# One layer of a hybrid streaming encoder: the DeltaNet heads' convolution copies on another engine, and their transposes placed at other k-tiles

## The chip, the core and the metric

The kernel runs on one core of one Trainium2 chip. The time is that of one execution on the device in microseconds; the median of three runs of the kernel before is 2997.08 us (2996.59 to 2997.41). One further execution was taken by the hardware profiler, and all rows in this document are from such profiled executions.

The core's engines each work through a queue of their own in order: PE (TensorE, matrix products and transposes; PEld is its weight load), DVE (VectorE), ACT (ScalarE), POOL (GpSimd) and SP, which only issues DMAs. They wait for one another through semaphores.

## The reference

One layer over 512 prompt frames and 64 sample frames, width 2048, all in float32. Cut to what matters here (the DeltaNet half, "GDN"; there is also a gated linear attention half, "GLA", and a gated feed-forward network behind both):

```python
mod = silu(c) @ w_ada + b_ada                       # 2048 x 12288, both conditions
h = rmsnorm(x, norm1) * (1 + sc1) + sh1
proj = h @ w_in                                     # 2048 x 7200
qkv, conv_new = causal_dwconv(concat([b_q, b_k, b_v]), st_conv, gdn_conv_w)   # 4 taps
qkv = silu(qkv)
q = l2norm(heads(c_q)) * 128 ** -0.5;  k = l2norm(heads(c_k));  v = heads(c_v)
...
lower = where(strict, einsum(kb, k) * decay, 0)     # per block
sol = triangular_solve(eye + lower, concat([v * beta, kb * exp(G)]))
u = sol_v - sol_k @ S
o = (q * exp(G)) @ S + (einsum(q, k) * decay) @ u
S = exp(G_last) * S + (k * exp(G_last - G)).T @ u
...
o = rmsnorm(o) * gain * silu(b_g)
x = x + g1 * (concat([o_gla, o_gdn]) @ w_out);  h = rmsnorm(x, norm2) * (1 + sc2) + sh2
x = x + g2 * ((silu(causal_dwconv(gate) + b) * val) @ w_down)
```

There are eight GDN heads of 128 columns. `conv_new`, the last three frames of the convolution's input for the prompt and for the sample, is an output.

## The kernel before

**Products.** Each float32 product is made of three products of a rounded upper half and a lower half: `split` loads a weight tile, ACT rounds it (L595, `wh`), DVE takes the rest (L596, `wl`), and `mm6` issues per k-tile of 128 six matmuls (two halves of the 576 frames, three products). `in_tile` makes one tile of 128 columns of the input projection from 16 k-tiles, and after each k-tile calls `tick`.

**Jobs.** The recurrence of a head runs as a Python generator (a job) between these k-tiles. `tick` calls `job_step` once per k-tile. It goes through the open jobs, the oldest first, and resumes each until one did work: a job that gives back `WAIT` lets the next one have the step as well. `rest(n)` gives back `WAIT` n times, so it is a pause of n k-tiles, longer where an older job works in between. `tick` also advances the modulation's blocks for later (`ada_block`, DVE at L738 and PE at L744).

`gdn_heads` makes the head's tiles in the order q(h+1), k(h+1), v(h), gate(h), 64 k-tiles a head; for head 0, q and k come from the stage before. After k(h) the job of head h is opened, so two jobs overlap. q, k and v each go through `gdn_conv`: ACT and DVE copy the projection out of PSUM into `cb` (L880, L881), with three columns in front of the prompt (zeros) and three in front of the sample (the state) from POOL (L882, L883); POOL copies the last three columns of both into `cs` (L884, L885); then ACT scales by the first tap (L886), DVE adds three taps (L888) and ACT applies Silu into the head's tile (L890) and the sample's (L891).

**The steps of a job** (`gdn`), where a `yield` ends a step:

- load of the decay rows `gb` by SP (L166), the masks `dl` and `du` on ACT (Relu, Exp) and POOL (`affine_select`, L174, L175);
- transposes of the raw keys (`transpose4`, L140, four per call, into one of four PSUM banks `bank`), squares on ACT, `rsqrt` (DVE adds at L133, POOL takes the power -1/2 at L134), scaled keys `kT`; one step; the same for the queries, of which only the lengths are kept; `rest(REST_T)`;
- `kn`, the transposes of `kT`; one step; `a` = keys by keys with the mask (L212); one step; keys by queries (L218); one step;
- `inverse16`: SP stores `a` to DRAM and loads its 16 x 16 diagonal blocks (a store and four loads), `rest(8)`, 14 steps with two POOL operations each (L343 to L350), a store (L351) and two loads on SP, two DVE operations that spread the result (L358), `rest(16)`;
- eight steps that double the inverse's block size to 128 (L234, L240, L249, L254);
- once the head's v is there: its transposes, then four blocks with two or three steps each (L272 to L301), whose outputs ACT collects in `ops`;
- squares of `ops`, `rsqrt`, scaling; `rest(REST_N)`; transposes of `ops` (L140), gain, gate, store.

A ninth job does the sample's frames of all heads, four GLA jobs and their sample job follow.

**Order.** The order on each engine's queue is fixed at compile time by the framework from priorities (program order) and its own estimate of durations; `high_priority` (AHEAD for weights, JOB_AHEAD for the jobs' ACT and DVE operations) moves instructions ahead by 80 places.

Helper lines: the jobs' ACT and DVE operations all carry L1584, so the tiles tell them apart (`m`, `sq`, `s`, `rq`). The widths of the pauses and the powers stand in these lines:

```python
REST_D, REST_X, REST_T, REST_N, REST_G = 8, 16, 3, 2, 3
self.nc.vector.tensor_scalar_add(out[:parts, :n], src[:parts, :n], EPS)
self.nc.gpsimd.tensor_tensor(out[:parts, :n], out[:parts, :n], self.mhalf[:parts, :n], op=ALU.pow)
```

Of the kernel before, what the change touches and what calls it, by code (L numbers as in the profile page):

```python
# [8 lines left out]
F32 = mybir.dt.float32  # L9
F32R = mybir.dt.float32r  # L10
I32 = mybir.dt.int32
AF = mybir.ActivationFunctionType
# [4 lines left out]
P = 128  # L17
# [14 lines left out]
JOB_RATE, ADA_RATE = 1.0, 0.65  # L32


REST_D, REST_X, REST_T, REST_N, REST_G = 8, 16, 3, 2, 3
LATE = 3
N_EARLY = 4
N_EXTRA = 24
# [53 lines left out]
class Kern:  # L92
# [58 lines left out]
    def gdn(self, qF, kF, x, gain, hcols, gb_src, s0, s_out, o_put, last_level):  # L151
# [7 lines left out]
        nc, c = self.nc, self.c  # L159
        V, A, T = self.jv, self.ja, nc.tensor  # L160
# [19 lines left out]
            A.activation(dl[:, b], dl[:, b], AF.Copy, scale=nbeta[:, b:b + 1])  # L180


        ss, rr = self.small(8), self.small(8)
        junk = self.half()
        kps = self.transpose4(kF)
        for b in range(4):
            A.activation(junk, kps[:, b], AF.Square, accum_out=ss[:, b:b + 1])
        self.rsqrt(rr, ss, 4)
        kT = self.m4()
        for b in range(4):  # L190
            A.activation(kT[:, b], kps[:, b], AF.Copy, scale=rr[:, b:b + 1])
        yield
        ss, rq = self.small(8), self.sp.tile([P, 4], F32, tag="rq", bufs=3, name=self.name("rq"))
        qps = self.transpose4(qF)
        for b in range(4):
            A.activation(junk, qps[:, b], AF.Square, accum_out=ss[:, b:b + 1])
        self.rsqrt(rq, ss, 4)
        V.tensor_scalar_mul(rq, rq, float(P) ** -0.5)
        yield from self.rest(REST_T)

        kn = self.m4()
# [21 lines left out]
        u, t = yield from self.inverse16(a)  # L223
# [83 lines left out]
        ss, rr = self.small(8), self.small(8)  # L307
        junk = self.half()
# [565 lines left out]
    def gdn_conv(self, ps, t, dst, name, h):  # L874

        nc = self.nc
        V, A = nc.vector, nc.scalar
        cb = self.ap.tile([P, 582], F32, tag="cb", bufs=1, name=self.name("cb"))
        acc = self.ap.tile([P, 582], F32, tag="ca", bufs=1, name=self.name("ca"))
        A.activation(cb[:, 3:515].rearrange("p (h t) -> p h t", h=2), ps[:, :, :HP], AF.Copy)  # L880
        V.tensor_copy(cb[:, 518:582].rearrange("p (h t) -> p h t", h=2), ps[:, :, HP:HT])  # L881
        nc.gpsimd.tensor_copy(cb[:, 0:3], self.zero3)  # L882
        nc.gpsimd.tensor_copy(cb[:, 515:518], self.vmap["st_conv"].rearrange("p (i t) -> p t i", i=3)[:, t])  # L883
        nc.gpsimd.tensor_copy(self.cs[:, 0, :, t], cb[:, 512:515])  # L884
        nc.gpsimd.tensor_copy(self.cs[:, 1, :, t], cb[:, 579:582])  # L885
        A.activation(acc[:, :579], cb[:, 0:579], AF.Copy, scale=self.vec("gdn_conv_w", t))  # L886
        for j in range(1, 4):
            V.scalar_tensor_tensor(acc[:, :579], cb[:, j:j + 579], self.vec("gdn_conv_w", 24 * j + t), acc[:, :579],  # L888
                                   op0=ALU.mult, op1=ALU.add)
        A.activation(dst, acc[:, 0:512], AF.Silu)  # L890
        self.put_s(name, h, lambda s: A.activation(s, acc[:, 515:579], AF.Silu))  # L891

    def put_o(self, k, t):
# [601 lines left out]
def layer_kernel(tc, i, o):  # L1495
    nc = tc.nc
    with ExitStack() as ctx:
        K = Kern(tc, ctx, i, o)
# [14 lines left out]
        with ExitStack() as early:  # L1513
            K.wp = pool(early, "wp", "right", bufs=3)
            with ExitStack() as right:
# [8 lines left out]
                K.mp = right.enter_context(_MixPool(tc))  # L1524
                with ExitStack() as st:
                    K.ap = pool(st, "ap", bufs=1)
                    K.jobs, K.at_job, K.at_ada = [], 0.0, 0.0
                    K.dp = dp
                    acc = [lambda n=n: K.ap.tile([P, 512], F32, tag=f"acc{n}", bufs=1, name=K.name("acc")) for n in range(2)]
# [116 lines left out]
```

## Time and profile before

| | |
|---|---|
| median of three runs | 2997.08 us |
| the profiled execution's own time | 3002.07 us |
| its span, first to last instruction | 3000.3 us |
| mean granted PE clock | 0.987 |
| busy: PE, DVE, ACT, POOL | 2912.2, 2095.7, 1242.9, 307.3 us |

The stages by time in the profile: the modulation, the norm and the first projections to about 150 us; the GDN heads to about 850; the GLA heads and half of the output projection to about 1400; the feed-forward network to the end.

How to read the rows. A group has its line, engine, operation, tiles (written `<-` read, buffer numbers left out), shapes and count, then busy time in us, mean ns of one, and the engine's idle time just before, with what ended it. A timeline row has start and duration in us, engine, line, operation and count, and in brackets the idle time before it with what ended that wait. A row of the waits has the waiting engine, tile and line, the releaser, then us in total, times and the longest. "PEq" or "SPq" is an engine's sequencer. "Granted clock" is the share of full speed that the throttle grants PE.

### The profile page before, as it was taken

How to read it: one execution, taken by the hardware profiler on the slowest of the kernel's cores; microseconds unless marked ns; L12 is line 12 of the kernel's file. 1: busy time of each engine (PE TensorE's matmuls, PEld its weight loads, DVE VectorE, ACT ScalarE, POOL GpSimd, SP SyncE). 2: the span in 40 equal slices, each digit the busy share in tenths (PEclk: the TensorE clock that was granted, in tenths of full speed). 3: DMA queues.
4: the chain of work that ended last, by engine and by line, in shares of the span. 5: the costliest groups of instructions: out<-in, count | busy, mean ns of one | idle time of the engine just before them, and what ended most of it. 6: DMA issues, size and time to landing. Idle time of an engine off the chain costs nothing.

```text
span 3000.3 us, 52414 instructions
## 1 busy us (share of the span) xinstructions
PE 2912.2 (97%) x21128; PEld 2796.7 (93%) x21128; DVE 2095.7 (70%) x3226; ACT 1242.9 (41%) x2116; POOL 307.3 (10%) x610
## 2 busy tenths in 40 slices
PE   7988999999999999999999999999999999999998
PEld 3588899999999998999999999999999999999998
DVE  5776667776578777367888888888888865555555
ACT  6555444554343333255444444444444432212223
POOL 0033333332200000000000000000000000000000
PEclk9999999999999999999999999999999999999999
DMA  7844545554455456543333333333333473333221
GB/s 274 283 142 134 148 121 149 144 152 134 133 144 145 135 159 172 153 143 96 97 111 105 106 98 111 106 104 99 112 104 104 122 238 101 116 101 106 89 85 65
DMA packets 532599, 392.95 MB, mean 131 GB/s; under 512 B 58729, under 2 KB 463204, under 8 KB 532356
## 3 DMA queue, kind: packets, MB, share of 16 engines
q1 hardware_dynamic: 532356, 389.59, 43.5%
q8 instruction: 167, 2.74, 0.4%
q14 instruction: 76, 0.62, 0.1%
HBM read 355.16 MB, written 34.36 MB: 130 GB/s over the span
## 4 chain that ended last, share of the span: by engine, by line
PE 65%; DVE 2%; DMA 1%; ACT 1%; issue 1%; POOL 0%; SPq 0%; ACTq 0%; POOLq 0%; DVEq 0%
PE g L508 19%; PE g L510 10%; PE g L1261 8%; PE g L1262 8%; PE g L1263 8%; PE bank L1262 3%; PE bank L1261 3%; PE bank L1263 3%; PE bank L401 1%; DVE acc L738 0%; PE bank L140 0%; PE bank L744 0%; PE bank L1471 0%; POOL s L134 0%; DMA xr<-od 0%
## 5 line engine op out<-in xcount | busy, mean ns | idle before, releaser
L508 PE MATMUL g<-slot,wh 128*128 128x288 f32 x3168 | 551.9, 295 | 0.2 <-DVE slot L1031 0.2
L1261 PE MATMUL g<-slot,wh 128*128 128x290 f32 x1760 | 533.6, 303 | 2.4 <-ACT p L1273 2.4
L1262 PE MATMUL g<-slot,wh 128*128 128x290 f32 x1760 | 526.1, 299 | 0.0
L1263 PE MATMUL g<-slot,wl 128*128 128x290 f32 x1760 | 521.2, 296 | 0.0
L595 ACT ACTIVATE wh<-raw 128x1024 fp32r<-128x1024 f32 x223 | 235.4, 1058 | 613.6 <-PE g L508 596.7
L508 PEld LDWEIGHTS g<-slot,wh 128*128 128x128 f32 x3168 | 466.2, 188 | 0.7 <-DVE slot L1031 0.5
L508 PE MATMUL g<-hh,wh 128*128 128x288 f32 x1984 | 453.7, 307 | 1.9 <-DVE cb L881 1.5
L510 PE MATMUL g<-hh,wl 128*128 128x288 f32 x1984 | 443.9, 302 | 3.4 <-DVE wl L596 3.4
L508 PE MATMUL g<-hl,wh 128*128 128x288 f32 x1984 | 439.8, 301 | 0.0
L1031 DVE SCALAR_TENSOR_TENSOR slot<-g,mod,slot 128x512 f32<-128x512 f32 (+1 forms) x448 | 201.9, 492 | 308.9 <-PE g L510 304.7
L738 DVE SCALAR_TENSOR_TENSOR acc<-xr,ct,acc 128x512 f32<-128x512 f32 x480 | 340.0, 754 | 35.4 <-DMA xr<-in_w_ada_dram 34.8
L1208 ACT ACTIVATE wh<-raw 128x1024 fp32r<-128x1024 f32 x176 | 186.7, 1061 | 393.5 <-PE g L1262 389.1
L1261 PEld LDWEIGHTS g<-slot,wh 128*128 128x128 f32 x1760 | 331.1, 188 | 16.7 <-ACT p L1273 11.5
L510 PE MATMUL g<-slot,wl 128*128 128x288 f32 x1584 | 343.2, 295 | 0.0
L1263 PEld LDWEIGHTS g<-slot,wl 128*128 128x128 f32 x1760 | 336.5, 191 | 0.0
L1262 PEld LDWEIGHTS g<-slot,wh 128*128 128x128 f32 x1760 | 334.6, 190 | 0.1
L508 PEld LDWEIGHTS g<-hh,wh 128*128 128x128 f32 x1984 | 324.3, 191 | 5.7 <-issue 1.6
L510 PEld LDWEIGHTS g<-hh,wl 128*128 128x128 f32 x1984 | 324.8, 191 | 4.3 <-DVE wl L596 3.7
L508 PEld LDWEIGHTS g<-hl,wh 128*128 128x128 f32 x1984 | 324.7, 191 | 1.0 <-issue 0.7
L596 DVE TENSOR_TENSOR wl<-raw,wh 128x1024 fp32r<-128x1024 f32 x223 | 272.3, 1222 | 58.6 <-ACT wh L595 57.9
L510 PEld LDWEIGHTS g<-slot,wl 128*128 128x128 f32 x1584 | 254.9, 188 | 0.0
L1209 DVE TENSOR_TENSOR wl<-raw,wh 128x1024 fp32r<-128x1024 f32 x176 | 214.9, 1221 | 19.8 <-ACT wh L1208 19.3
(367 smaller groups left out, 4415.7 us busy)
## 6 DMA issues: line engine op xcount, KB each, us to landing
raw<-in_w_up_dram SPq DMA_DIRECT2D x176, 512.0 KB
xr<-in_w_ada_dram SPq DMA_DIRECT2D x128, 512.0 KB
raw<-in_w_in_dram SPq DMA_DIRECT2D x108, 512.0 KB
raw<-in_w_down_dram SPq DMA_DIRECT2D x88, 512.0 KB
hraw<-in_w_ada_dram SPq DMA_DIRECT2D x64, 512.0 KB
raw<-in_w_out_dram SPq DMA_DIRECT2D x32, 512.0 KB
slot<-actd SPq DMA_DIRECT2D x44, 288.0 KB
actd<-v SPq DMA_DIRECT2D x44, 256.0 KB
```

What stands on the lines that cost most here:

```text
L401: T.matmul(ps[:, b * 64:(b + 1) * 64], e3[:, b], qc[:, b * 64:(b + 1) * 64], start=True, stop=True)
L508: T.matmul(ps[:, h if bank is None else bank, :n], wh, x[:, h, :n], start=f, stop=False)
L510: T.matmul(ps[:, h if bank is None else bank, :n], wl, ah[:, h, :n], start=False, stop=stop)
L595: nc.scalar.activation(hi[:, :n_], raw[:, :n_], AF.Copy)
L596: nc.vector.tensor_tensor(lo[:, :n_], raw[:, :n_], hi[:, :n_].bitcast(F32), op=ALU.subtract)
L738: V.scalar_tensor_tensor(acc[s], w[:, k], col, acc[s], op0=ALU.mult, op1=ALU.add)
L1031: self.nc.vector.scalar_tensor_tensor(x1[:, :, z], ps[:, :, c], gain[:, q:q + 1], x1[:, :, z], op0=ALU.mult, op1=ALU.add)
L1208: self.nc.scalar.activation(hi, src, AF.Copy)
L1209: self.nc.vector.tensor_tensor(lo, src, hi.bitcast(F32), op=ALU.subtract)
L1261: T.matmul(ps, wh[:, j], hi, start=(c < 3 and j == 0), stop=False, skip_group_check=True)
L1262: T.matmul(ps, wh[:, j], lo, start=False, stop=False, skip_group_check=True)
L1263: T.matmul(ps, wl[:, j], hi, start=False, stop=(j == NPAIR - 1), skip_group_check=True)
```

## The change

Four edits, all in the GDN heads:

- the convolution's four POOL copies: the zeros in front of the prompt are written once into a tile `gcb` that all convolutions share; the state in front of the sample and the two copies into `cs` become ACT operations, the latter two behind the first Silu;
- a new pause of six k-tiles (REST_C) between the masks and the first transposes of a job;
- one `rsqrt` of eight columns for the lengths of keys and queries, behind the queries' squares, with the scaled keys after it;
- REST_T from 3 to 6 and REST_N from 2 to 6.

```diff
-REST_D, REST_X, REST_T, REST_N, REST_G = 8, 16, 3, 2, 3
+REST_D, REST_X, REST_T, REST_N, REST_G = 8, 16, 6, 6, 3
+REST_C = 6
...
+        yield from self.rest(REST_C)
         ss, rr = self.small(8), self.small(8)
+        rq = self.sp.tile([P, 4], F32, tag="rq", bufs=3, name=self.name("rq"))
         junk = self.half()
         kps = self.transpose4(kF)
         for b in range(4):
             A.activation(junk, kps[:, b], AF.Square, accum_out=ss[:, b:b + 1])
-        self.rsqrt(rr, ss, 4)
+        yield
+        qps = self.transpose4(qF)
+        for b in range(4):
+            A.activation(junk, qps[:, b], AF.Square, accum_out=ss[:, 4 + b:5 + b])
+        self.rsqrt(rr, ss, 8)
+        V.tensor_scalar_mul(rq, rr[:, 4:8], float(P) ** -0.5)
         kT = self.m4()
         for b in range(4):
             A.activation(kT[:, b], kps[:, b], AF.Copy, scale=rr[:, b:b + 1])
-        yield
-        ss, rq = self.small(8), self.sp.tile([P, 4], F32, tag="rq", bufs=3, name=self.name("rq"))
-        qps = self.transpose4(qF)
-        for b in range(4):
-            A.activation(junk, qps[:, b], AF.Square, accum_out=ss[:, b:b + 1])
-        self.rsqrt(rq, ss, 4)
-        V.tensor_scalar_mul(rq, rq, float(P) ** -0.5)
         yield from self.rest(REST_T)
...
-        cb = self.ap.tile([P, 582], F32, tag="cb", bufs=1, name=self.name("cb"))
+        cb = self.gcb
...
-        nc.gpsimd.tensor_copy(cb[:, 0:3], self.zero3)
-        nc.gpsimd.tensor_copy(cb[:, 515:518], self.vmap["st_conv"].rearrange("p (i t) -> p t i", i=3)[:, t])
-        nc.gpsimd.tensor_copy(self.cs[:, 0, :, t], cb[:, 512:515])
-        nc.gpsimd.tensor_copy(self.cs[:, 1, :, t], cb[:, 579:582])
+        A.activation(cb[:, 515:518], self.vmap["st_conv"].rearrange("p (i t) -> p t i", i=3)[:, t], AF.Copy)
         A.activation(acc[:, :579], cb[:, 0:579], AF.Copy, scale=self.vec("gdn_conv_w", t))
...
         A.activation(dst, acc[:, 0:512], AF.Silu)
+        A.activation(self.cs[:, 0, :, t], cb[:, 512:515], AF.Copy)
+        A.activation(self.cs[:, 1, :, t], cb[:, 579:582], AF.Copy)
...
+                    K.gcb = K.ap.tile([P, 582], F32, tag="cb", name="gcb")
+                    nc.scalar.activation(K.gcb[:, 0:3], K.zero3, AF.Copy)
```

## The prediction

> **What bounds the kernel now.** I read the whole page first, then the busy time by stage, then the waits of TensorE (PE) in the one stage that the diff touches, and last the timelines of the engines around the longest of those waits. The page and the stage view:
>
> ```profile
> span 3000.3 us, 52414 instructions
> ```
> ```profile
> 150.00:850.00 700.00, 657.19 (x4864) 629.87 (x4864) 466.11 (x787) 338.55 (x851) 209.53 (x410) 0.96 0.49 141
> ...
> 850.00:1400.00 550.00, 539.86 (x3988) 524.17 (x3986) 376.38 (x684) 219.50 (x392) 17.01 (x44) 1.00 0.50 143
> ```
>
> The columns are the stretch and its length, then busy time of PE, PEld, DVE, ACT and POOL, then granted clock, DMA share and GB/s. PE is what the end waits for, so only PE's lost time can be won. In 150 to 850 us, where the DeltaNet jobs run between the projection's matmuls, PE idles 700 - 657.2 = 42.8 us and is granted 0.96 of its clock; afterwards it idles 10 us in 550 at full clock. Who ends those idle times, in the waits of PE in this stretch (total, times, longest):
>
> ```profile
> PE bank L140 <- ACT m L1584: 25.1, 13, 9.1
> PE bank L140 <- ACT qkv L890: 5.2, 3, 2.8
> PE g L510 <- DVE wl L596: 3.4, 1, 3.4
> PE bank L240 <- DVE m L1584: 3.4, 3, 1.4
> ```
>
> L140 is `transpose4`. The row "ACT m" holds the transposes of scaled keys (`kn`) and of the outputs (`ops`); the row "ACT qkv" those of raw keys, which wait for the convolution's Silu (L890). Together 30.3 us. They stand in PE's queue before their data is there, and the matmuls behind them stand with them.
>
> **Why they wait.** First the outputs, in the timelines of POOL, ACT and PE (start, duration, what; in brackets the idle time before):
>
> ```profile
> 398.13 3.01 POOL L882 COPY cb<-zero 128x3 f32<-128x3 f32 x1 [3.63 <-DVE ca L888]
> ...
> 401.20 0.12 POOL L343 MEMSET m<- 32x16 f32 x1
> ...
> 415.39 0.59 POOL L350 COPY m<-m 32x256 f32<-32x256 f32 x1
> 415.95 1.01 POOL L134 TENSOR_TENSOR s<-s,mhalf 128x4 f32<-128x4 f32 x1
> ```
> ```profile
> 416.99 1.28 ACT L1584 ACTIVATE m<-m,s 128x128 f32<-128x128 f32 x4 [5.72 <-POOL s L134]
> ```
> ```profile
> 417.45 0.48 PE L140 MATMUL bank<-consts,m 128*128 128x128 f32 x1 [4.76 <-ACT m L1584]
> ```
>
> The power of the output norm (L134) starts the moment the next job's 16-block inverse leaves POOL (L343 to L350, 401.20 to 415.98, 14.8 us). That inverse had itself no idle time before it: it stood behind a three-element copy of the convolution that waited 3.63 us and then took 3.01. Second, the longest wait (SP, ACT, PE):
>
> ```profile
> 223.44 0.33 SPq L351 DMA_DIRECT2D d<-m  x1
> ...
> 228.09 1.23 SPq L166 DMA_DIRECT2D m<-gd  x1
> ```
> ```profile
> 233.69 0.99 ACT L1584 ACTIVATE m<-m,ncum 128x128 f32<-128x128 f32 x3 [0.71 <-DMA m<-gd]
> ...
> 240.19 1.10 ACT L1584 ACTIVATE m<-bank,s 128x128 f32<-128x128 f32 x4
> ```
> ```profile
> 240.59 0.47 PE L140 MATMUL bank<-consts,m 128*128 128x128 f32 x1 [9.10 <-ACT m L1584]
> ```
>
> SP cannot issue job 1's load of decay rows (L166) until job 0's inverse result (L351) has gone out; ACT builds job 1's masks from 233.69 and only at 240.19 scales its keys. Third, raw keys:
>
> ```profile
> 366.18 0.63 ACT L890 ACTIVATE qkv<-ca 128x512 f32<-128x512 f32 x1 [2.60 <-DVE ca L888]
> ```
> ```profile
> 366.86 1.09 PE L140 MATMUL bank<-consts,qkv 128*128 128x128 f32 x8 [2.77 <-ACT qkv L890]
> ```
>
> **The pauses.** One step of a job is one k-tile, six matmuls of one form. Six matmuls further, the timeline of PE has the same pair again:
>
> ```profile
> 360.88 0.43 PE L508 MATMUL g<-hh,wh 128*128 128x288 f32 x2
> ...
> 361.67 0.43 PE L508 MATMUL g<-hh,wh 128*128 128x288 f32 x2
> ```
>
> A k-tile is 0.79 us. So REST_C puts 6 x 0.79 = 4.7 us of other matmuls ahead of raw keys; the longest wait there is 2.8, so all 5.2 us should go. REST_N from 2 to 6 adds 3.2 us ahead of the output transposes. REST_T from 3 to 6 adds 2.4 ahead of `kn`.
>
> The pauses also change whose steps come first, and this I count from the code, with a job's start as step 0 and 64 steps between starts (two stages of a job overlap with the older job, which goes first). Before: raw keys 0, queries 1, the older job's inverse levels 2 to 10, `kn` 12, `a` 13, the older job's values 16 to 28 with its output power, its output transposes 30. PE's own order agrees (the eight transposes of raw keys and queries, the levels, `kn`):
>
> ```profile
> 451.86 1.09 PE L140 MATMUL bank<-consts,qkv 128*128 128x128 f32 x8
> 452.79 1.00 PE L234 MATMUL bank<-m,m 128*128 128x64 f32 x8
> ...
> 463.96 0.66 PE L140 MATMUL bank<-consts,m 128*128 128x128 f32 x4
> ```
>
> After: raw keys 6, queries 7, older levels 11 to 19, older values 19 to 31, `kn` 33, `a` 34, older outputs 37. Two consequences. `kn` comes 26 steps behind the queries instead of 11, so it cannot be late in the steady state. And `a`, which feeds the inverse, comes after the older job's output power instead of before it, so that power no longer queues behind the 14.8 us. The wait of 4.76, of which the pause alone would leave 4.76 - 3.2 = 1.6, should therefore go too. With `a`, the five DMAs that carry it to the inverse, the store and two loads that carry the result back, all on SP, come 21 steps later; the levels that use them come 9 steps later, so they keep 41 steps (32 us of k-tiles alone) for the 14.8 us and the DMAs.
>
> Only jobs 0 and 1 lack this. Job 0 starts without an older job: its `kn` moves from step 5 to 14 and its inverse by the same 9 steps, 7 us. Job 1's `kn` moves from 37 to 46, 9 steps as well, so the inverse of job 0 and job 1's keys shift together. What helps there is that the load of decay rows is asked for at step 33 as before, now ahead of L351, and that POOL has less to do. Bounds for job 1: from nothing left to all 9.1 left. I take 2.5, nearer to the lower end, because the masks come out of the chain if SP's order follows the steps.
>
> **POOL's copies and the power** (groups of POOL and one of ACT: busy us, mean ns, idle before):
>
> ```profile
> L882 POOL COPY cb<-zero 128x3 f32<-128x3 f32 x23 | 23.3, 1014 | 91.8 <-DVE ca L888 84.8 <-ACT wh L595 3.6 <-ACT m L1584 3.4
> L134 POOL TENSOR_TENSOR s<-s,mhalf 128x4 f32<-128x4 f32 x18 | 22.1, 1229 | 103.7 <-DVE s L133 103.7
> L885 POOL COPY cs<-cb 128x3 f32<-128x3 f32 x24 | 14.0, 584 | 14.2 <-DVE cb L881 12.7
> ...
> L883 POOL COPY cb<-cols 128x3 f32<-128x3 f32 x23 | 10.4, 454 | 0.0
> L884 POOL COPY cs<-cb 128x3 f32<-128x3 f32 x24 | 10.3, 431 | 128.6 <-ACT cb L880 128.6
> ```
> ```profile
> L838 ACT ACTIVATE egs<-last 128x4 f32<-128x4 f32 x1 | 0.2, 196 | 0.0
> ```
>
> Four copies for each of 24 convolutions leave POOL: 58 us of work, and, worth more, some 230 us in which POOL stood waiting at them, whatever came next behind it. Three of the four come back on ACT, 72 x 0.196 = 14.1 us (nearest row: 128x4). ACT is busy 338.55 us of 700, so this lies beside other work; the bounds are 0 and 14.1, and as only the copy ahead of L886 lies in the convolution's own chain, I take 0.5. The merged power, eight columns for twice four, has no row: it lies between one power of 1.23 us and two, 2.46. Either way the keys' scaling now waits for the queries' squares too, 3 us at most, with 26 steps of cover (6 for jobs 0 and 1, inside their 2.5).
>
> **The clock.** After the waits PE is granted half its clock (same columns as the stage view):
>
> ```profile
> 240.60:245.00 4.40, 4.40 (x19) 4.40 (x20) 0.00 (x0) 4.28 (x10) 0.00 (x0) 0.50 0.00 0
> ...
> 367.90:374.70 6.80, 6.80 (x33) 6.78 (x32) 2.13 (x4) 2.31 (x14) 1.01 (x1) 0.50 0.29 80
> ...
> 417.45:422.45 5.00, 5.00 (x22) 4.98 (x23) 2.19 (x4) 1.51 (x4) 0.00 (x0) 0.50 0.86 209
> 423.00:428.00 5.00, 5.00 (x40) 5.00 (x39) 4.21 (x6) 0.99 (x1) 0.00 (x0) 1.00 0.95 306
> ```
>
> Five microseconds hold 22 matmuls at half clock and 40 at full, so a half-clock microsecond loses 0.45. The three stretches are 16.2 us: 7.3 us go with the waits that caused them. [...]
>
> **The sum.** Gone: 25.1 + 5.2 + 7.3 = 37.6. Left or new: 2.5 (job 1), 0.5 (ACT), 3.0 for waits in a new order (the size of one of the two single-cause rows that nothing addresses, 3.4 each), 1.0 of clock on these; 7.0. Gain 30.6. The profiled execution took 3002.07 us (span 3000.3 and 1.77 around it), the median of the runs is 2997.08, 5.0 lower: 3002.07 - 30.6 = 2971.5 in the profile's terms, 2966 in the median's.
>
> **The rivals.** *The inverse's result becomes the wait.* From `a` to the levels there were 53 steps, now 41. DVE already stands at the first use of that result:
>
> ```profile
> DVE m L358 <- DMA cm<-d: 21.4, 5, 8.3
> ```
>
> DVE serves its queue in order, and the lower halves of the weights (L596) are behind L358. If half of the 21.4 us reaches PE, with clock at 0.45, that is 15.5 us and the time is 2982. For it: the wait of 3.4 us for L596 shows that PE has little weight in stock. Against: five such waits today fall on no wait of PE for L596.
>
> *The order does not follow the pauses.* The order on each engine is planned at compile time from estimated times; if PE's transposes are placed by estimated readiness, the pauses change little: 2997. Against it stands PE's order above.
>
> *Slower.* The bank of raw keys now stays taken until the merged power, and there are four such banks for all jobs. If the power falls into the older job's inverse, as the output power does now, the bank stays for up to 14.8 us and PE waits for a bank. It decides from the point where the inverse ends after the power:
>
> ```profile
> 488.22 0.59 POOL L350 COPY m<-m 32x256 f32<-32x256 f32 x1
> ...
> 528.32 1.44 POOL L134 TENSOR_TENSOR s<-s,mhalf 128x4 f32<-128x4 f32 x1 [0.33 <-DVE s L133]
> ```
>
> Today 39.5 us lie between them. `a` moves 21 steps, the power 7: 14 steps of 73 us / 64 (the distance of the L350 rows of two jobs, 488.22 - 415.39) take away 16 us, and 23 remain, so I hold it unlikely. If it happened at four of the heads, each would wait 14.8 less the 4.7 of a pause, 10 us, 40 in all, and some 9 of clock: 49 lost against 37.6 won, 3008.
>
> *More goes.* Waits that nothing addresses vanish with the new order: all 42.8 idle and the clock with it, about 2948.
>
> **How the numbers follow.** Forecast 0.62, with its own range 2959 (nothing left, nothing new) to 2981 (job 1 keeps 9.1, ACT costs 2, new waits 8, 3 of clock on them); inverse's result 0.18; order unchanged 0.07; slower 0.09; more 0.04. The predicted time is the likeliest case's 2966. The range 2952 to 2988 takes in the forecast, the first rival and, at its lower end, a part of the last case, about 0.8. Within 0.2% (6 us, about what a measurement of this kernel can tell from no change) lies the unchanged order and a sliver of the first rival, 0.08; slower 0.09; faster 0.83.
>
> **What would show it.** Right: no wait of PE at L140 above 1 us in 150 to 850 save at job 1; output powers on POOL before the next inverse's memset, not after L350; granted clock 0.98 or more; the same stage some 30 us shorter, the later ones unchanged. Wrong: PE waiting for a bank while the merged power stands behind L350; PE waiting for L596 while DVE stands at L358; L140 waits of the same total at other places.

## The result and the profile after

The changed kernel takes 3026.48 us (median of four runs, 3023.60 to 3029.94), the kernel before 2996.84 in the runs beside it: the ratio is 1.0102, with 95% interval 1.0085 to 1.0120. It is 30 us slower, where 31 us faster was forecast. The profiled execution took 3023.60 us with a span of 3021.9, 21.6 above the span before.

The stage view with the two stretches that were shown of before (the stretch and its length, busy time of PE, PEld, DVE, ACT and POOL, granted clock, DMA share, GB/s):

```profile
150.00:850.00 700.00, 641.01 (x4730) 618.10 (x4728) 452.01 (x753) 337.58 (x895) 160.44 (x306) 0.96 0.48 136
850.00:1400.00 550.00, 540.84 (x3977) 521.26 (x3977) 374.02 (x681) 213.41 (x392) 15.36 (x38) 0.99 0.51 146
```

PE now idles 700 - 641.0 = 59.0 us in the DeltaNet stage, 16 more than before, and gets 134 matmuls less done in it; POOL is busy 49 us less, as meant. The loss is made here and nowhere else: the matmul of the projection that starts at 992.4 us before starts at 1015.4 after, and from there on the distance stays within 2 us. Over that stretch (from the projection's matmul at 163.36 us before and 163.98 after) PE's idle time grew from 41.9 to 59.8 us, and the time at half clock from 51.2 to 68.3 us. At the 0.45 of the prediction the latter is 7.7 us of work; together 25.6, against 22.3 by which the stretch is longer.

PE's waits in 150 to 850 us (total, times, longest), with `transpose4` now at L141 and the jobs' helper line at L1586:

```profile
PE bank L141 <- ACT m L1586: 12.6, 3, 11.0
PE bank L141 <- ACT qkv L888: 12.5, 5, 5.4
PE bank L241 <- DVE m L1586: 11.1, 4, 7.8
PE bank L213 <- ACT m L1586: 5.3, 7, 0.9
PE g L511 <- DVE wl L597: 4.4, 4, 1.6
PE g L509 <- DVE gcb L882: 3.1, 3, 1.8
PE bank L141 <- DMA qkv<-sd_k: 2.7, 1, 2.7
PE g L509 <- ACT wh L596: 2.7, 1, 2.7
```

The first row was 25.1 with 13 waits. What is left of it is one wait of 11.0 at job 1's `kn`, 1.3 at job 0's and nothing of note at output transposes: those went, as forecast. But raw keys went from 5.2 to 12.5 although a pause of six k-tiles now stands ahead of them, the inverse's levels (L241) from 3.4 to 11.1, `a` (L213) from nothing to 5.3, the weights' halves and the convolution together from 5.3 to 10.2, and the sample's keys wait 2.7 for a load that is new in the list.

**Why raw keys wait longer.** The timelines of SP, ACT, DVE and PE at the longest of these waits (start, duration, what; in brackets the idle time before):

```profile
352.78 0.33 SPq L352 DMA_DIRECT2D d<-m  x1
...
355.98 0.38 SPq L167 DMA_DIRECT2D m<-gd  x1
```
```profile
359.40 0.99 ACT L1586 ACTIVATE m<-m,ncum 128x128 f32<-128x128 f32 x3 [8.85 <-DMA m<-gd]
...
365.91 0.57 ACT L881 ACTIVATE gcb<-g 128x512 f32<-128x512 f32 x1
...
372.18 0.63 ACT L888 ACTIVATE qkv<-ca 128x512 f32<-128x512 f32 x1 [1.64 <-DVE ca L886]
```
```profile
357.44 1.29 DVE L359 TENSOR_TENSOR m<-cm,consts 128x512 f32<-128x512 f32 x2 [8.76 <-DMA cm<-d]
...
366.52 0.23 DVE L882 COPY gcb<-g 128x64 f32<-128x64 f32 x1 [6.64 <-ACT gcb L881]
```
```profile
372.86 1.97 PE L141 MATMUL bank<-consts,qkv 128*128 128x128 f32 x8 [5.41 <-ACT qkv L888]
```

Read from the top: SP can store the result of the older job's inverse only at 352.78, when POOL has it. The next job's decay rows stand behind that store. ACT stands 8.85 us for them and then builds masks until 366; the convolution's first copy (L881) is behind the masks, so Silu comes at 372.18, and PE's transposes wait, pause or not. DVE, too, stands 8.76 us at the spread of the inverse's result. Before, the inverse of this job ended at 333.9 (the tile that POOL copies last, L350), now at 352.8; for the next four jobs 416.0, 488.8, 559.5, 630.1 became 433.3, 512.8, 588.6, 667.4. The waits of ACT and DVE over the stage:

```profile
ACT m L1586 <- DMA m<-gd: 62.3, 8, 12.1
```
```profile
DVE m L359 <- DMA cm<-d: 56.8, 9, 12.6
```

The first was 26.6 before, the second 21.4. After each of the next four inverses the same two waits stand together (ACT 8.54 to 11.79 us for the decay rows, DVE 4.57 to 9.24 at the spread), and PE's raw-key waits of 3.88 and 2.03 us come behind the first two of these. The longest wait at a level has the same head, seen on SP, ACT, DVE and PE; between them stand the masks, then the weight's upper half (L596), which DVE's lower half waits for:

```profile
753.44 0.47 SPq L167 DMA_DIRECT2D m<-gd  x1
```
```profile
760.58 0.99 ACT L1586 ACTIVATE m<-m,ncum 128x128 f32<-128x128 f32 x3 [12.15 <-DMA m<-gd]
...
767.33 1.04 ACT L596 ACTIVATE wh<-raw 128x1024 fp32r<-128x1024 f32 x1
```
```profile
768.40 1.23 DVE L597 TENSOR_TENSOR wl<-raw,wh 128x1024 fp32r<-128x1024 f32 x1 [8.79 <-ACT wh L596]
```
```profile
770.11 1.94 PE L241 MATMUL bank<-m,m 128*128 128x64 f32 x8 [7.78 <-DVE m L1586]
```

**Job 1.** Its 11.0 us, on POOL, ACT and PE:

```profile
226.52 0.62 POOL L351 COPY m<-m 32x256 f32<-32x256 f32 x1
227.12 0.62 POOL L176 TENSOR_SCALAR_AFFINE_SELECT m<-m 128x512 f32<-128x512 f32 x1
...
235.41 2.56 POOL L135 TENSOR_TENSOR s<-s,mhalf 128x8 f32<-128x8 f32 x1 [7.08 <-DVE s L134]
```
```profile
227.78 1.28 ACT L1586 ACTIVATE m<-m,nbeta 128x128 f32<-128x128 f32 x4 [7.30 <-POOL m L176]
```
```profile
238.42 0.48 PE L141 MATMUL bank<-consts,m 128*128 128x128 f32 x1 [11.03 <-ACT m L1586]
```

The decay rows do come early (issued at 209.56 in place of 228.09). But the masks' `affine_select` stands on POOL behind job 0's inverse, which now falls just there; ACT waits 7.30 us for it with the squares, a convolution copy and two weight casts behind, and then the eight-column power takes 2.56 us. POOL's queue, too, holds the next job behind an inverse.

### The profile page after: what moved, and what is told of

Read it like the earlier page. It is cut to its first block, busy times and chain, and to the rows that moved or that the text cites. A ratio compares the mean times of both kernels' runs of the same rounds, so it can differ in the third digit from the quotient of the medians.

```text
span 3021.9 us, 52345 instructions
## 1 busy us (share of the span) xinstructions
PE 2918.0 (97%) x21128; PEld 2803.1 (93%) x21128; DVE 2094.9 (69%) x3217; ACT 1250.4 (41%) x2188; POOL 259.4 (9%) x505
## 4 chain that ended last, share of the span: by engine, by line
PE 80%; DVE 5%; POOL 4%; DMA 4%; ACT 3%; issue 2%; SPq 0%; ACTq 0%; POOLq 0%; DVEq 0%
PE g L509 25%; PE g L511 12%; PE g L1261 8%; PE g L1262 8%; PE g L1263 8%; PE bank L1262 3%; PE bank L1261 3%; PE bank L1263 3%; DVE acc L739 2%; POOL m L349 2%; POOL m L348 1%; PE bank L141 1%; ACT m L1586 1%; POOL s L135 1%; DMA xr<-in_w_ada_dram 1%
## 5 line engine op out<-in xcount | busy, mean ns | idle before, releaser
L596 ACT ACTIVATE wh<-raw 128x1024 fp32r<-128x1024 f32 x223 | 235.5, 1058 | 620.4 <-PE g L509 590.7
L1209 DVE TENSOR_TENSOR wl<-raw,wh 128x1024 fp32r<-128x1024 f32 x176 | 214.7, 1220 | 20.2 <-ACT wh L1208 19.5
```

What stands on the lines that cost most here:

```text
L596: nc.scalar.activation(hi[:, :n_], raw[:, :n_], AF.Copy)
L1209: self.nc.vector.tensor_tensor(lo, src, hi.bitcast(F32), op=ALU.subtract)
```

## The experiments

Theory 1: the longer pauses put `a` behind the older job's values, the inverse starts and ends later, and what waits for it holds up everything behind it on SP, ACT and DVE, and at job 1 on POOL. Rivals: ACT's new copies; the merged power; the pauses by their mere length; any move away from the old places. "Theory 2" in the texts below is ACT's copies in e1 to e4, and the pauses in themselves in e16, e19 and e15. The times are medians, the ratios those to the kernel before, measured beside the run; 0.1% is 3.0 us. "us slower" below goes by the ratio.

| run | kernel | us | before | ratio, 95% interval |
|---|---|---|---|---|
| e1_copies | before + copies on ACT | 2999.97 | 3000.39 | 0.9999, 0.9988 to 1.0010 |
| e2_pauses | before + pauses | 3034.10 | 3000.39 | 1.0116, 1.0094 to 1.0137 |
| e3_c0t3 | after, REST_C 0, REST_T 3 | 3022.49 | 3000.39 | 1.0071, 1.0052 to 1.0090 |
| e4_c0 | after, REST_C 0 | 3034.00 | 3000.39 | 1.0111, 1.0090 to 1.0132 |
| e6_n6 | before + REST_N 6 | 3006.13 | 3002.22 | 1.0008, 0.9995 to 1.0021 |
| e10_merge | before + merged power | 3018.27 | 3002.22 | 1.0045, 1.0027 to 1.0064 |
| e8_d1pool | after, store on POOL's queue | 3034.39 | 3002.22 | 1.0098, 1.0082 to 1.0113 |
| e11_before_d1pool | before, the same | 3001.41 | 3002.22 | 1.0002, 0.9990 to 1.0015 |
| e16_t4 | before + REST_T 4 | 3018.62 | 3002.10 | 1.0050, 1.0035 to 1.0065 |
| e19_pauses_first | e2 + younger job first | 3023.27 | 3002.10 | 1.0072, 1.0056 to 1.0088 |
| e15_first | after + younger job first | 3023.70 | 3002.10 | 1.0071, 1.0056 to 1.0086 |
| e17_sp_free | after, store and loads on POOL's queue | 3027.93 | 3002.10 | 1.0085, 1.0066 to 1.0104 |
| e20_first_sp | e19 + the same | 3015.13 | 3004.12 | 1.0046, 1.0030 to 1.0061 |
| e21_before_sp | before + the same | 3031.51 | 3004.12 | 1.0103, 1.0082 to 1.0123 |
| e24_sep | after, two powers | 3034.93 | 3004.12 | 1.0109, 1.0092 to 1.0126 |
| e22_first_t3 | a version meant to be faster | 3031.24 | 3004.12 | 1.0099, 1.0075 to 1.0122 |
| e25_inv_late | before, inverse's steps 13 later | 3005.56 | 3002.07 | 1.0016, 1.0004 to 1.0029 |
| e26_inv_early | before, inverse's steps 6 earlier | 3008.02 | 3002.07 | 1.0023, 1.0008 to 1.0038 |

### The parts one by one

**e1_copies**: of the change only the convolution's part.

```diff
-        cb = self.ap.tile([P, 582], F32, tag="cb", bufs=1, name=self.name("cb"))
+        cb = self.gcb
-        nc.gpsimd.tensor_copy(cb[:, 0:3], self.zero3)
-        nc.gpsimd.tensor_copy(cb[:, 515:518], self.vmap["st_conv"].rearrange("p (i t) -> p t i", i=3)[:, t])
+        A.activation(cb[:, 515:518], self.vmap["st_conv"].rearrange("p (i t) -> p t i", i=3)[:, t], AF.Copy)
...
-        nc.gpsimd.tensor_copy(self.cs[:, 0, :, t], cb[:, 512:515])
+        A.activation(self.cs[:, 0, :, t], cb[:, 512:515], AF.Copy)
```

> Only the convolution's copies move from POOL to ACT (shared tile gcb); pauses and the two powers as before. Theory 1 (late inverse: the pauses REST_C and REST_T put `a` behind the older job's values, the inverse ends later, and what stands behind its result on SP, ACT and DVE is late): the copies are harmless, 2985 to 2998 us. Theory 2 (the copies on ACT make the convolution late in ACT's queue, and so the raw keys): slower than before, 3008 or more, with raw-key waits of 10 us or more in total.

No difference that can be measured. Freeing POOL of its 94 small copies is worth nothing and costs nothing here; the rival of ACT's copies falls. So does the worth that the prediction saw in the 230 us for which POOL stood at these copies: with them gone PE still waits 26.1 us at `transpose4` for ACT (25.1 before).

**e2_pauses**: of the change only the pauses.

```diff
-REST_D, REST_X, REST_T, REST_N, REST_G = 8, 16, 3, 2, 3
+REST_D, REST_X, REST_T, REST_N, REST_G = 8, 16, 6, 6, 3
+REST_C = 6
...
+        yield from self.rest(REST_C)
         ss, rr = self.small(8), self.small(8)
```

> Only the pauses (6, 6, 6); copies on POOL and two powers as before. Theory 1: as slow as the changed kernel or slower, 3018 to 3040 us, with the inverse's end 18 us or more later in each head than before and DVE standing 40 us or more at the spread of its result. Theory 2: the loss is gone, below 3000.

35 us slower: the pauses alone lose as much as the whole change (the intervals overlap). The inverses of jobs 2 to 6 end at 358, 439, 512, 591 and 671 us, 23 to 41 us later than before, and DVE stands 59.7 us at the spread; both are as theory 1 expected. At job 1 the raw keys wait 10.55 us, behind masks for which ACT stands 9.64 us until POOL is through with job 0's inverse.

**e6_n6**: only the pause ahead of output transposes, `REST_N` 6 in the kernel before.

> The kernel before with REST_N 6 alone. If a later place of the output transposes is only cover for them, their waits (14 us before) shrink and nothing else moves: 2978 to 2994 us. If REST_N is what keeps the kernel with REST_C 0 and REST_T 3 slow (it had output waits of 12 and 7 us), 3010 or more.

Neutral, between the two expectations, and the waits it was to remove are still there; the longest ends at 426.92 us and is 12.70 long. (The traced execution took 3012.21 us, the median is 3006.13.) There POOL stood 7.31 us for the first half of the `rsqrt`, which stands on DVE behind L738, and L738 waited 10.66 us for a block of w_ada. A pause of 3.2 us does not cover such a wait.

**e10_merge**: only the merged power, at the old pauses.

```diff
-        self.rsqrt(rr, ss, 4)
...
+            A.activation(junk, qps[:, b], AF.Square, accum_out=ss[:, 4 + b:5 + b])
+        self.rsqrt(rr, ss, 8)
+        V.tensor_scalar_mul(rq, rr[:, 4:8], float(P) ** -0.5)
```

> The kernel before with the merged power alone (keys are scaled only after the queries' squares). If the merged power is what keeps the kernel with REST_C 0 and REST_T 3 slow, by making the keys, `a` and the inverse late: 3008 to 3025 us, and `a` of job 0 some 6 to 8 us later than before. If not: 2994 to 3004.

13 us slower. Most of it is not at `kn`, where the power is needed, but at output transposes: three of them wait 4.43, 10.37 and 8.25 us where the kernel before has 2.96, 4.76 and 2.59. The longest, on SP, DVE and PE (here L350 is the store of the inverse's result, L729 the load of w_ada, L133 the first half of the output's `rsqrt`):

```profile
415.72 0.33 SPq L350 DMA_DIRECT2D d<-m  x1
416.13 0.38 SPq L729 DMA_DIRECT2D xr<-in_w_ada_dram  x1
```
```profile
420.16 0.75 DVE L737 SCALAR_TENSOR_TENSOR acc<-xr,ct,acc 128x512 f32<-128x512 f32 x1 [9.24 <-DMA xr<-in_w_ada_dram]
...
422.89 0.16 DVE L133 TENSOR_SCALAR s<-s 128x4 f32<-128x4 f32 x1
```
```profile
425.06 0.47 PE L140 MATMUL bank<-consts,m 128*128 128x128 f32 x1 [10.37 <-ACT m L1583]
```

A load that has nothing to do with the inverse stands behind its store on SP; DVE stands 9.24 us for that load, and L133 stands behind that. DVE at the same head of the kernel before:

```profile
411.88 0.27 DVE L133 TENSOR_SCALAR s<-s 128x4 f32<-128x4 f32 x1
...
420.26 2.74 DVE L738 SCALAR_TENSOR_TENSOR acc<-xr,ct,acc 128x512 f32<-128x512 f32 x4 [8.12 <-DMA xr<-in_w_ada_dram]
```

There SP has the same two DMAs in the same order (416.01 and 416.43), and DVE stands 8.12 us for the load as well. But L133 is done before that wait. So the 5.6 us more of PE at this head go with the place of one small operation on DVE, ahead of or behind an instruction that waits; in e6 L133 stands behind it too (423.54).

**e24_sep**: the changed kernel with the two powers of before put back (the reverse of the diff above).

> The changed kernel with the keys' and the queries' own powers put back: what is left of the change is the pauses and the copies. If the late inverse carries the loss and the merged power adds nothing once it is there: 3024 to 3036 us, as with the pauses alone (3034) and with the whole change (3026). If the merged power's 13 us are a part of the whole change's 30: 3010 to 3020.

As slow as the pauses alone: once the pauses are there, the merged power adds nothing that can be measured. The 13 us and the 35 us are not terms of one sum.

### Which pause, and by how much

**e3_c0t3** and **e4_c0**: the changed kernel with `REST_C` 0 and `REST_T` 3, and with `REST_C` 0 alone.

> The changed kernel with REST_C 0 and REST_T 3; REST_N 6, copies on ACT and the merged power stay. Theory 1: `a` is back at step 13, the loss goes and the gain of the output transposes stays: 2972 to 2990 us. Theory 2 or a theory that the merged power is late: 3010 or more.

> The changed kernel with REST_C 0 alone; REST_T stays 6. Counted by steps, `kn` comes at 15, but `a` only at 28, behind the older job's values, which is 6 steps before where the changed kernel has it and 15 behind where it was. Theory 1: most of the loss stays, 3005 to 3022 us. A theory by which each step of pause costs its share (6 of the 9): 2990 to 3004. Theory 2: unchanged, 3026.

Taking away REST_C gains nothing; taking REST_T back to 3 as well gains some 9 to 12 us. Both are slower than theory 1 expected, e3 by 32 us or more. What is left in e3, 21 us, is somewhat more than the merged power costs alone, and stands at the same output transposes: 4.83, 12.04 and 7.43 us.

**e16_t4**: one line, `REST_T` 4 in the kernel before.

> The kernel before with REST_T 4 instead of 3, nothing else. By the count of steps this one step is enough to put the DMA that carries `a` to the inverse behind the older job's values phase: it goes from step 15 to step 28, while `kn` and `a` move by one step only (13, 14). Theory 1 (the inverse that starts and ends late is what costs): the inverses of jobs 2 to 6 end some 10 us or more later than before, the waits of DVE at the spread of its result and of ACT for the decay rows grow, and the time is 8 to 30 us above the kernel before. Theory 2 (each pause costs by its length, whatever it does to the order): one step of 0.79 us at each job changes nothing that can be measured, within 5 us.

One k-tile costs 15 us (the traced execution took 3009.71 us, the median is 3018.62, so the trace shows only some 8 of them). The size is theory 1's, but the place is not: the waits of DVE at the spread and of ACT for the decay rows did not grow (17.8 and 14.4 us). The inverse ended 5 to 7 us later at jobs 2 to 4 (3 to 4.5 of these are `a` itself), and the older job's output power, which in the kernel before already started the moment the inverse left POOL, came later with it (at job 3 three operations before its end). Job 4's inverse and job 3's output power on POOL, then job 3's output transposes on PE, of e16 and of the kernel before:

```profile
495.26 0.59 POOL L350 COPY m<-m 32x256 f32<-32x256 f32 x1
495.82 1.01 POOL L134 TENSOR_TENSOR s<-s,mhalf 128x4 f32<-128x4 f32 x1
```
```profile
497.32 0.48 PE L140 MATMUL bank<-consts,m 128*128 128x128 f32 x1 [8.05 <-ACT m L1584]
```
```profile
490.28 0.33 PE L140 MATMUL bank<-consts,m 128*128 128x128 f32 x1 [2.59 <-ACT m L1584]
```

At the three heads where this happens the waits were 2.96, 4.76 and 2.59 us, and are 6.61, 6.35 and 8.05: 10.7 us of PE. About half of this is PE's own order: counted by the projection's matmuls, these transposes stand 1 to 3.5 k-tiles nearer to `a` than before. The other half is the inverse. The kernel before stands where the inverse ends just as the output power is due, so what comes later there is paid at once; the full pauses jump over that place (the output power is ahead of the inverse) and pay at the next head's start.

### Is it the late inverse?

**e19_pauses_first** and **e15_first**: pauses alone, and the whole change, with the younger job served first until its `a` has been sent.

```diff
+        self.first = True
         yield from self.rest(REST_C)
...
-        u, t = yield from self.inverse16(a)
+        inv = self.inverse16(a)
+        next(inv)
+        self.first = False
+        yield WAIT
+        u, t = yield from inv
...
-        for g in list(self.jobs):
+        for g in self.jobs[::-1] if self.first else list(self.jobs):
```

> The kernel before with all three pauses (C 6, T 6, N 6), as in the run that was 34 us slower, but from its start until its `a` has been sent to the inverse the younger job is served ahead of the older one. By the count `kn` then stands at step 13, `a` at 14 and its DMA at 16, as before the change (12, 13, 15). Theory 1: the inverse is early again, its ends are back near those of the kernel before (334, 416, 489 us), most of the 34 us come back, and the time is within 10 us of the kernel before. Theory 2 (the pauses cost in themselves, because banks and buffers stay taken longer): still 25 us or more above the kernel before.

> The changed kernel with the same rule: the younger job goes first until its `a` has been sent. Theory 1: what is left of the loss is the merged power's part, which was 13 us by itself, so 5 to 18 us above the kernel before, and less than the changed kernel's 30. Theory 2: as the changed kernel, 25 us or more above the kernel before.

The inverses of jobs 2 to 6 end at 327, 409, 491, 568 and 643 us in e19, near those of before, ACT's waits for the decay rows fall to 2.6 us, and the time comes down by 13 us against e2. That is much less than theory 1 asked: 22 us are left, with an interval (17 to 26) that takes in theory 2's 25 at its end. In e15 the inverses are back too (338, 416, 495, 571 and 642 us), and the time is 21 us above the kernel before, again between the two theories. PE's waits of e19 say where much of the rest is (L286 is the older job's values phase), besides 10.56 us at job 1's raw keys, which the rule does not move:

```profile
PE bank L286 <- DVE sq L1591: 19.6, 4, 9.4
```
```profile
413.75 0.75 DVE L745 SCALAR_TENSOR_TENSOR acc<-xr,ct,acc 128x512 f32<-128x512 f32 x1 [10.15 <-DMA xr<-in_w_ada_dram]
```
```profile
414.81 0.80 PE L286 MATMUL bank<-sq,m 128*128 128x128 f32 x2 [9.35 <-DVE sq L1591]
```

The early inverse now ends in the middle of the older job's values, and SP's store (409.16) again has a load of w_ada behind it (409.54). As in e10, the kernel before has that wait of DVE as well; what is new is the work that stands behind it.

### Is it SP's queue?

**e8_d1pool** and **e11_before_d1pool**: the store of the inverse's result issued by POOL, in the changed kernel and in the kernel before.

```diff
-        nc.sync.dma_start(d1.rearrange("w q f -> q w f"), lane)
+        nc.gpsimd.dma_start(d1.rearrange("w q f -> q w f"), lane)
```

> The changed kernel, with the store of the inverse's result (d1) issued from POOL's queue, behind the operation that makes it, in place of SP's. Theory 1a (SP stands at this store until POOL has finished, and the next job's decay rows and the weights of projection and modulation stand behind it): waits of ACT for the decay rows fall from 62 to below 25 us, raw-key waits of PE from 12.5 to below 5, and the time to 2985 to 3010. If the late inverse costs through its result alone (DVE at the spread, levels): no more than 8 us gained, 3018 or more.

> The kernel before with the same store on POOL's queue. Theory 1a: SP's waits at this store (72 us) go, the waits of PE at L140 for ACT fall from 25 to below 15, 2975 to 2993 us. If SP's order is harmless in the kernel before: 2995 to 3005.

Nothing changed, but nothing was freed either, so this tests neither theory. SP now waits at the next instruction, the load of what was stored, as SP's waits of e8 show:

```profile
SPq L355 <- DMA d<-m: 86.4, 9, 13.8
```

**e17_sp_free, e20_first_sp, e21_before_sp**: the two loads behind it as well, in the changed kernel, in e19 and in the kernel before.

```diff
-            nc.sync.dma_start(cm[:, w], d1[w].rearrange("(b n) (i j) -> (n i) b j", b=4, i=16))
+            nc.gpsimd.dma_start(cm[:, w], d1[w].rearrange("(b n) (i j) -> (n i) b j", b=4, i=16))
```

> The changed kernel with the store of the inverse's result and the two loads behind it issued from POOL's queue, so that SP's queue waits for the inverse nowhere. If the late inverse costs through SP's queue (the decay rows, weights and w_ada loads that stand behind the store), the load of the decay rows is no longer late, ACT's waits for them fall from 62 us to under 15, and the time falls by 10 us or more against the changed kernel. If it costs through DVE, which still stands at the spread until the result has landed, the waits at the spread stay near 57 us and the time stays within 6 us of the changed kernel.

> The run with all pauses and the younger job first, once more, but with the store of the inverse's result and the two loads behind it on POOL's queue. In the trace of that run the inverses were early again, yet PE lost 19.1 us in three waits for DVE at the values phase of the older job (L286: 3.04, 6.68, 9.35), and the longest of them stands at 405 us, where DVE waits 10.15 us for a load of w_ada that stands on SP behind the store of the inverse's result (issued 409.16 and 409.54). Theory SP (the rest of the pauses' loss comes through SP's queue, which the store holds until the inverse ends): those waits go, DVE's waits for w_ada fall from 32 to under 12 us, and the time falls from 21 to 0 to 10 us above the kernel before. Rival (every move away from the tuned order costs as much in some other wait): still 15 us or more above.

> The kernel before with the same three transfers on POOL's queue, nothing else. Theory SP: DVE's waits for w_ada (31.6 us) and ACT's for the decay rows (26.6 us) fall to under 15 us each, the wait of 9.1 us at job 1's keys shrinks, and the time falls by 5 to 20 us. Rival: the waits go elsewhere (POOL now stands at the transfers, its powers come later) and the time stays within 5 us.

In the changed kernel (e17) ACT's waits for the decay rows fall from 62.3 to 19.3 us, DVE's at the spread rise from 56.8 to 65.0, and no gain can be told (the interval reaches 1.0066 to 1.0104, the changed kernel's 1.0085 to 1.0120). The longest wait at raw keys and the longest at a level, both followed above to the decay rows, are gone, but other raw keys wait, with DVE's spread ahead of their convolution, and the total is 12.2 us against 12.5. The raw keys of the head shown above, then DVE and PE at the longest raw-key wait of e17 (between the two ACT stands 6.01 us for DVE's part of the convolution's copy, at 687.63):

```profile
372.99 1.07 PE L141 MATMUL bank<-consts,qkv 128*128 128x128 f32 x8
```
```profile
678.08 1.73 DVE L359 TENSOR_TENSOR m<-cm,consts 128x512 f32<-128x512 f32 x2 [8.57 <-DMA cm<-d]
```
```profile
696.61 1.97 PE L141 MATMUL bank<-consts,qkv 128*128 128x128 f32 x8 [5.59 <-ACT qkv L888]
```

So SP's queue alone is not what binds: freed of the inverse, it leaves DVE's. What the transfers cost POOL in e17 isn't separated from that. In e20 the waits at L286 are down to 0.8 us, and the time is 8 us lower than in e19, with intervals that overlap a little; 14 are left, between the two expectations, with 11.40 us at job 1's raw keys and 25.3 at `transpose4` for ACT in PE's waits. In the kernel before (e21) the waits that the edit aimed at went as expected (DVE's for w_ada from 31.6 to 9.5 us, ACT's for the decay rows from 26.6 to 7.3), and yet it costs 31 us: POOL now stands at the transfers with the output power behind them, and PE's waits at `transpose4` for ACT go from 25.1 to 54.4 us. Job 3's inverse on POOL with job 2's output power, and its output transposes on PE:

```profile
423.31 0.59 POOL L350 COPY m<-m 32x256 f32<-32x256 f32 x1
424.20 0.62 POOL L351 DMA_DIRECT2D d<-m  x1 [0.30 <-POOL m L350]
426.72 1.52 POOL L354 DMA_DIRECT2D cm<-d  x2 [1.89 <-issue]
428.25 1.05 POOL L134 TENSOR_TENSOR s<-s,mhalf 128x4 f32<-128x4 f32 x1
```
```profile
429.80 0.47 PE L140 MATMUL bank<-consts,m 128*128 128x128 f32 x1 [10.68 <-ACT m L1584]
```

From the end of the inverse to the power there are 4.3 us in which POOL issues the transfers or stands at them; before there was nothing. The store takes POOL 0.62 us, where it took SP 0.33 at 352.78 in the changed kernel.

### The inverse's steps alone

**e25_inv_late** and **e26_inv_early**: the kernel before with `REST_D`, `REST_X` = 21, 3 and 2, 22 in place of 8, 16.

> The kernel before with REST_D 21 in place of 8 and REST_X 3 in place of 16: the 16-block inverse alone starts 13 steps later; raw keys, queries, `kn`, `a`, the levels that use its result, the values and the output transposes keep the steps they had. If a late inverse costs by itself (through DVE at the spread, SP behind the store and ACT behind the decay rows), the inverses end some 10 us or more later and the time is 10 to 35 us above the kernel before. If it is the order of PE's own transposes that costs, nothing of it is moved here and the time is within 5 us.

> The kernel before with REST_D 2 and REST_X 22: the inverse alone 6 steps (4.7 us of k-tiles) earlier, all else at its step. If only lateness costs, the time is within 6 us of the kernel before or below it. If any move away from the tuned places costs, it is 8 us or more above.

Both are within 7 us of the kernel before (5 and 7 us slower by the ratio), but neither is a test: against its `a` the inverse was not moved. Job 3's `a` on PE (L212) and the start of its inverse on POOL (L343), of e25:

```profile
392.65 1.73 PE L212 MATMUL bank<-m 128*128 128x128 f32 x8
```
```profile
406.76 0.12 POOL L343 MEMSET m<- 32x16 f32 x1
```

14.1 us lie between them; in e26 it is 14.3 (384.76 to 399.08), in the kernel before 14.2 (387.01 to 401.20). So POOL's start does not follow these two pauses, and a late inverse by itself was not tried.

### A version meant to beat both

**e22_first_t3**: the kernel before with the copies on ACT, `REST_N` 6, the younger job first and the three transfers on POOL's queue.

> A version without the late inverse and without SP's wait: the kernel before with the copies off POOL, REST_N 6, no pause ahead of raw keys and REST_T 3, two powers, the younger job first until its `a` is sent (by the count `kn` at step 4, `a` 5, its DMA 7 in place of 12, 13, 15) and the inverse's result on POOL's queue. Theory SP and theory 1 together: the inverse ends earlier than before, none of its waits is left, and the time is 5 to 25 us below the kernel before. Rival: `kn` at step 4 is too early for ACT, PE waits at L140 for scaled keys at every job, and the time is 5 us or more above the kernel before.

30 us slower. DVE stands 58.5 us at the spread and PE 21.4 us for DVE in the values phase. No version here is faster than the kernel before; e1, e6 and e11 equal it within what can be measured.

## Why the prediction was wrong

**The output transposes: right.** The output power now precedes the next inverse, as argued. Job 2's power and the next inverse's start, of the changed kernel:

```profile
411.41 1.38 POOL L135 TENSOR_TENSOR s<-s,mhalf 128x4 f32<-128x4 f32 x1 [22.25 <-DVE s L134]
420.03 0.12 POOL L344 MEMSET m<- 32x16 f32 x1 [7.24 <-DMA m<-d]
```

PE's waits at output transposes went with it. By e6 the pause of 3.2 us alone does not do that; that the order on POOL does is read from these rows.

**The step that failed** is the sentence on `a` and the inverse: that they come 21 steps later, that the levels come 9 steps later, and that they "keep 41 steps (32 us of k-tiles alone) for the 14.8 us and the DMAs". The count of `a`'s steps was right (in PE's order it comes 19.5 to 21 k-tiles later at jobs 3 to 7, 15.5 at job 2), and so was the conclusion for the levels' own data: no wait at their first products (L235) stands in PE's list. But it asked only whether the result is there when PE uses it, not what stands in each queue behind the instructions that wait for it: SP's store with the decay rows and weights behind, ACT's masks with convolution and casts behind, DVE's spread. The pauses alone cost 35 us (e2), where they were costed at nothing. In the terms of the sum it is the 3.0 us for waits in a new order: the rows that stand for it grew by 20.6 (levels 7.7, `a` 5.3, the weights' halves and the convolution 4.9, the sample's keys 2.7). The waits at `transpose4`, 30.3 in the sum, are 29.0 in all, at other places, the last of the prediction's signs of being wrong. The first rival named one of these queues (DVE at L358, with the lower halves behind) and took half of 21.4 us; DVE's wait became 56.8 us, and that rival left SP, ACT and POOL out. The case called slower came out in its sign alone: in the changed kernel no merged power stands behind the older job's inverse on POOL in the steady state, and no wait for a bank behind it is in PE's list.

**Raw keys: wrong.** "4.7 us of other matmuls ahead" was to cover a wait of 2.8. The convolution ahead of them became later by more than the pause, 5.41 us at the longest wait.

**Job 1: 2.5 expected, 11.0 found.** The decay rows came early, as the step said. The masks did not leave the chain, because two of their operations are on POOL, behind job 0's inverse; POOL's queue was not looked at for them. And job 1's `kn` was to come 9 steps later; in PE's order it stands 4 k-tiles earlier, so PE stood at it from 227.4 us on (231.5 before), and ACT scaled the keys at 238.00 (240.19 before).

**The merged power** was "3 us at most, with 26 steps of cover". Within the change that held (e24), and its 1.94 us on average lie inside the bounds. By itself it costs 13 us, at other places than its own.

**ACT's copies: right**, 0.5 forecast and no difference measured; their duration of 0.2 us each as well.

**The clock** was to give back 7.3 us and cost 7.7 instead, as the waits grew. The three pieces in the sum were 16.2 of the 51.2 us that the stage spent at half clock before.

**What stays open.** The pauses are shown to carry the loss (e2, e24), one k-tile of REST_T to cost 15 us by itself (e16), and the order of the jobs to give back 13 of the 35 us (e19 against e2). That the inverse's place does it, through the queues of SP, ACT, DVE and POOL, is read from the traces, and e17 bears it out for SP at the two chains followed above. No run moved the inverse alone, and how the loss divides among the queues wasn't settled: e17 freed SP and gained nothing clear of noise, e20 freed it and gained a little, and both put the transfers on POOL, which has a price of its own (4.3 us at the head shown of e21). Every version that moved `kn` or `a`, or put all three transfers on POOL's queue, was 13 to 35 us slower, each with other waits; that rival, any move away from the tuned places, is not excluded.

## What to carry to other kernels

A pause in front of an instruction that waits is a move of everything the job issues behind it; cost it at the slowest chain that it moves (here an inverse on another engine with a round trip through DRAM), and for each instruction that waits for that chain, list what stands behind it in its queue, whatever it belongs to. A long wait on a queue may cost nothing as it is (DVE's 8.12 us in the kernel before), and cost PE as soon as an operation that PE needs slips behind it (5.6 us more at that head in e10). Where PE is busy 97% of the span and the pauses have been set by hand, change one place at a time: one k-tile in one pause cost 15 us here, two edits that cost 13 and 35 us alone cost 30 together, and the copies, which leave the jobs' steps where they were, cost nothing.

## What the hardware showed

From 150 to 850 us of the two traces half clock came in pieces of 3.4 us or multiples of it (3.4, 6.8, 10.2 and 13.7), also after short waits. The kernel before at a level that waited 1.36 us, then the stage view just before and in the piece:

```profile
813.28 0.96 PE L240 MATMUL bank<-m,m 128*128 128x64 f32 x7 [1.36 <-DVE m L1584]
```
```profile
811.80:814.90 3.10, 1.74 (x14) 1.65 (x14) 1.76 (x3) 0.00 (x0) 0.00 (x0) 1.00 0.80 242
815.00:818.40 3.40, 3.40 (x18) 3.39 (x16) 0.00 (x0) 0.38 (x1) 0.00 (x0) 0.50 1.06 326
```

In the 3.1 us before the piece PE was busy for 1.74. So a wait of 1.4 us can cost 1.4 + 3.4 x 0.45 = 2.9 us of PE, an estimate from these rows and the 0.45 of the prediction. It need not: after the wait of 2.96 us that ends at 335.37 in the kernel before, the granted clock is 1.00 from 332 to 340 us.
